# Linear attention with each head's decayed queries in a column block of their own, the other head's rows zero

## The chip, the cores and the metric

The kernel runs on one core of a Trainium2 chip. The metric is the device time of one execution in microseconds (us). The core has five engines that run side by side: TensorE (PE; its weight loads are listed apart as PEld), VectorE (DVE), ScalarE (ACT), GpSimd (POOL) and SyncE (SP), which here issues the transfers. TensorE multiplies a stationary operand, loaded as weights, with a moving operand that streams through column by column; the contraction runs over the partitions, that is the rows of its array, and results go to PSUM.

## The reference

Two layers of a hybrid block over 256 context and 1024 latent positions. Each layer projects a normalized input, runs three branches (gated linear attention, grouped-query attention, a recurrent branch) and merges them. The change is in the first branch, in fp32 throughout:

```python
q_dec = q * jnp.exp(g_cum)
k_inv = k * jnp.exp(-g_cum)
k_tail = k * jnp.exp(g_last - g_cum)
lower = jnp.tril(jnp.ones((GLA_CHUNK, GLA_CHUNK), bool))
a = jnp.where(lower, jnp.einsum('bhncd,bhnsd->bhncs', q_dec, k_inv), 0.0)
o = jnp.einsum('bhncs,bhnse->bhnce', a, v)
u = jnp.einsum('bhncd,bhnce->bhnde', k_tail, v)
decay = jnp.exp(g_last[:, :, :, 0, :])
...
o = o + jnp.einsum('bhncd,nbhde->bhnce', q_dec, s_in)
```

There are 4 heads with 64 key and 128 value elements, each run forward and backward over the positions; the two directions are added, normalized and gated.

## The kernel before, in words

`hybrid_kernel` goes through the two layers (L339). In a layer the linear attention comes early. For each pair of heads (`for g in range(2)`, L657) `gla_proj` (L528) makes queries `rq`, keys `rk` and values `v` for the pair, and `gla_core` (L541) does the attention. `weave` (L203) emits the core with high priority and puts attention projections (`att_proj`, L649) between its steps; the order on every engine's queue is then planned for the whole program from the emitted order, the priorities and estimated times. Behind the second pair come the projections of the recurrent branch (`rwkv_proj`), the attention, the recurrent branch itself (`gram`, `merge`, `chain`) and the merge of the branches.

In the core a pair of heads lies on the partitions: head 0 on rows 0 to 63, head 1 on rows 64 to 127, and the 1280 positions along the columns. For each direction `d`, the cumulated gates `G` are made, their exponentials `Ep` and `Em` (L575, L576), the decayed queries `qd[d]` (L584) and keys `kd[d]` (L585). For d = 0 these are tiles of their own; for d = 1 the queries are multiplied in place in `rq`, the keys in `rk`. `kt` is the transposed keys, and `R[d]` the states at the start of each tile of 128 positions, built one tile after the other on TensorE, VectorE and GpSimd (L596 to L603).

Then the tile loop (L605) goes over the tiles of 128 positions: 10 in layer 0, the 8 latent ones in layer 1, so with two pairs 36 tiles in all. Per tile:

- queries times keys, L616 to L620: for each direction and head a product on the head's 64 rows, [64 x 128] by [64 x 128], into the columns 128d of one PSUM buffer per head (`pa`);
- the mask, L622: one VectorE instruction per head, both directions, into `aT`;
- `aT` times values, L627, on 128 rows, into one PSUM buffer per head (`po`);
- queries times state, L631, on the head's 64 rows, added into the same buffer;
- the norm and the gate (L633 to L638), two transposes of the result `gth` through PSUM `u` (L642), a scaled copy, and the transfer to memory (L646).

The PSUM tag `a` has two buffers (L115), which `pa` and `po` and the state products take in turn. Fp32 products appear in the trace as two MATMUL instructions each, transposes as one; all products are recorded under L85 and all transposes under L90, the lines of the helper class.

Of the kernel before, what the change touches and what calls it, by code (L numbers as in the profile page):

```python
# [9 lines left out]
F32 = mybir.dt.float32  # L10
F32R = mybir.dt.float32r
AF = mybir.ActivationFunctionType
ALU = mybir.AluOpType
# [7 lines left out]
NT = CTX + SEQ  # L21
# [49 lines left out]
def hybrid_kernel(ctx: ExitStack, tc: tile.TileContext, I: dict, C: dict, out: bass.AP):  # L71
# [3 lines left out]
    vec = nc.vector  # L75
    pool = nc.gpsimd
# [16 lines left out]
    pe = PE  # L93

    def nm(s):
        cnt[0] += 1
        return f"{s}{cnt[0]}"
# [3 lines left out]
    def popen(**kw):  # L101
        g = tc.tile_pool(bufs=1, reuse_waits="tile", **kw)
        open_pools.append(g)
        return g, g.__enter__()
# [12 lines left out]
    def ps(tag):  # L117
        return psp.tile([128, 512], F32, tag=tag, bufs=PSB[tag], name=nm("ps_" + tag))
# [7 lines left out]
    def dense():  # L126
        ring["i"] += 1
        return ps(ring["tags"][(ring["i"] - 1) % len(ring["tags"])])
# [18 lines left out]
    for j in range(2):  # L147
        vec.tensor_scalar(
            out=sil[:, :, j, :], in0=cth[:, j, :].unsqueeze(2).to_broadcast([128, 8, 16]),
# [189 lines left out]
    for l in range(DEPTH):  # L339
# [57 lines left out]
        def th512():  # L397
            return ta.tile([128, 512], F32, tag="th", bufs=3, name=nm("th"))
# [22 lines left out]
        if l + 1 < DEPTH:  # L421
            mpool, mp = popen(name=nm("modp"))
            md, _ = modulation(l + 1, mp, 2)
# [83 lines left out]
        gpool, gp_ = popen(name=nm("gp"))  # L507
        glow, ge = popen(name=nm("ge"))
# [3 lines left out]
        amask = gp_.tile([128, 256], F32, name="amask")  # L512
# [15 lines left out]
        def gla_proj(pr):  # L528
# [9 lines left out]
                pass  # L538
            return qk, vt

        def gla_core(pr, qk, vt):  # L541
            qd, kd, R = {}, {}, {}
            for d in range(2):
                G = ge.tile([128, NT], F32, tag="G", bufs=2, name=nm("G"))
                for (t0, n) in BLK:
                    pz = ps("a")
                    pe.matmul(pz[:, :n], wup[96:128, d, 128 * pr:128 * pr + 128], wd[96:128, t0:t0 + n], start=True, stop=True)
                    ab = ge.tile([128, 512], F32, tag="ab", bufs=1, name=nm("ab"))
                    act(out=ab[:, :n], in_=pz[:, :n], func=AF.Abs, bias=bz[:, d, pr:pr + 1])
                    act(out=ab[:, :n], in_=ab[:, :n], func=AF.Exp, scale=-1.0)  # L550
                    act(out=ab[:, :n], in_=ab[:, :n], func=AF.Ln, bias=1.0)
                    mn = th512()
                    vec.tensor_scalar(out=mn[:, :n], in0=pz[:, :n], scalar1=bz[:, d, pr:pr + 1], scalar2=0.0, op0=ALU.add, op1=ALU.min)
                    pool.tensor_tensor(out=mn[:, :n], in0=mn[:, :n], in1=ab[:, :n], op=ALU.subtract)
                    go, gi = G[:, t0:t0 + n], mn[:, :n]
                    if d:
                        go, gi = go[:, ::-1], gi[:, ::-1]
                    for i in range(0, n, 128):
                        vec.tensor_tensor_scan(out=go[:, i:i + 128], data0=one.to_broadcast([128, 128]), data1=gi[:, i:i + 128], initial=0.0, op0=ALU.mult, op1=ALU.add)
                    yield 0.5  # L560
                G3 = G.rearrange("p (t c) -> p t c", c=128)
                mid = 64 if d else 63
                last = 0 if d else 127
                em = small.tile([128, NTILE, 1], F32, tag="em", bufs=2, name=nm("em"))
                act(out=em, in_=G3[:, :, mid:mid + 1], func=AF.Exp, scale=1.0 / 16)
                vec.tensor_copy(out=(gm := small.tile([128, NTILE, 1], F32, tag="gm", bufs=2, name=nm("gm"))), in_=G3[:, :, mid:mid + 1])
                vec.tensor_tensor(out=G3, in0=G3, in1=gm.to_broadcast([128, NTILE, 128]), op=ALU.subtract)
                if d == 0:
                    qd[d] = Ep = gp_.tile([128, NT], F32, tag="qd", name=nm("qd"))
                    kd[d] = Em = gp_.tile([128, NT], F32, tag="kd", name=nm("kd"))  # L570
                else:
                    Ep = ge.tile([128, NT], F32, tag="G", bufs=2, name=nm("E"))
                    Em = G
                    qd[d], kd[d] = qk["q"], qk["k"]
                act(out=Ep, in_=G, func=AF.Exp, scale=1.0 / 16)  # L575
                act(out=Em, in_=G, func=AF.Exp, scale=-1.0 / 16)  # L576
                order = list(range(NTILE)) if d == 0 else [1, 0] + list(range(9, 1, -1))
                cf = small.tile([128, NTILE, 1], F32, tag="cf", bufs=2, name=nm("cf"))
                eL = Ep.rearrange("p (t c) -> p t c", c=128)[:, :, last:last + 1]
                for i in range(NTILE - 1):  # L580
                    a, b = order[i], order[i + 1]
                    vec.tensor_tensor(out=cf[:, a], in0=eL[:, a], in1=em[:, b], op=ALU.mult)
                q0 = 0 if need_ctx else CTX
                vec.tensor_tensor(out=qd[d][:, q0:], in0=Ep[:, q0:], in1=qk["q"][:, q0:], op=ALU.mult)  # L584
                vec.tensor_tensor(out=kd[d], in0=Em, in1=qk["k"], op=ALU.mult)  # L585
                kt = ge.tile([128, NTILE, 128], F32, tag="G", bufs=2, name=nm("kt"))
                for t0 in range(0, NTILE, 4):
                    m = min(4, NTILE - t0)
                    pt = ps("u")
                    for i in range(m):  # L590
                        pe.transpose(pt[:, 128 * i:128 * i + 128], kd[d][:, 128 * (t0 + i):128 * (t0 + i) + 128], ident)
                    act(out=kt[:, t0:t0 + m, :].rearrange("p t c -> p (t c)"), in_=pt[:, :128 * m], func=AF.Copy)
                    yield 0.5
                R[d] = gp_.tile([128, NTILE, 128], F32, tag=f"R{d}", name=nm("R"))
                vec.memset(R[d][:, order[0], :], 0.0)
                for i in range(NTILE - 1):  # L596
                    a, b = order[i], order[i + 1]
                    pu = ps("a")
                    for h in range(2):
                        pe.matmul(pu[64 * h:64 * h + 64, 0:128], kt[:, a, 64 * h:64 * h + 64], vt[:, a, 128 * h:128 * h + 128], start=True, stop=True)  # L600
                    rt = ge.tile([128, 128], F32, tag="rt", bufs=1, name=nm("rt"))
                    vec.tensor_tensor(out=rt, in0=pu[:, 0:128], in1=R[d][:, a, :], op=ALU.add)
                    pool.tensor_scalar(out=R[d][:, b, :], in0=rt, scalar1=cf[:, a], scalar2=None, op0=ALU.mult)  # L603
                    yield 0.45
            for t in tiles:  # L605
                c = slice(128 * t, 128 * t + 128)
# [4 lines left out]
                pool.tensor_scalar(out=yo, in0=yo, scalar1=1.0, scalar2=None, op0=ALU.add)  # L611
                vec.reciprocal(out=yo, in_=yo)
                pool.tensor_tensor(out=th, in0=th, in1=yo, op=ALU.mult)
                aT = gp_.tile([128, 2, 256], F32, tag="aT", bufs=2, name=nm("aT"))

                pa = [ps("a"), ps("a")]  # L616
                for d in range(2):
                    for h in range(2):
                        r = slice(64 * h, 64 * h + 64)
                        pe.matmul(pa[h][:, 128 * d:128 * d + 128], kd[d][r, c], qd[d][r, c], start=True, stop=True)  # L620
                for h in range(2):
                    vec.scalar_tensor_tensor(out=aT[:, h], in0=pa[h][:, 0:256], scalar=3e38, in1=amask, op0=ALU.min, op1=ALU.mult)  # L622
                po = [ps("a"), ps("a")]
                for h in range(2):
                    vv = vt[:, t, 128 * h:128 * h + 128]
                    for d in range(2):
                        pe.matmul(po[h][:, 0:128], aT[:, h, 128 * d:128 * d + 128], vv, start=d == 0, stop=False)  # L627
                for d in range(2):
                    for h in range(2):
                        r = slice(64 * h, 64 * h + 64)  # L630
                        pe.matmul(po[h][:, 0:128], qd[d][r, c], R[d][r, t, :], start=False, stop=d == 1)  # L631
                ss = small.tile([128, 2], F32, tag="ss2", name=nm("ss2"))
                for h in range(2):  # L633
                    act(out=yo[:, 128 * h:128 * h + 128], in_=po[h][:, 0:128], func=AF.Square, accum_out=ss[:, h:h + 1])
# [22 lines left out]
        for g in range(2):  # L657
            banks("mm", "mm", "o")
            pj = gla_proj(g)
            banks("mm", "mm", "o")  # L660
            weave(gla_core(g, *pj), att_proj(g), 1.0, None, 3000)
# [632 lines left out]
        for bi, wo in enumerate(("w_o_gla", "w_o_att", "w_o_rwkv")):  # L1294
            if bi == 2:
                mb = blocks_of(blks)
            for jj in range(4):
                wh, wl = load_w([I[wo][l, :, 256 * jj:256 * jj + 256]], kt=4)
                for j in range(2):
                    kr = 2 * jj + j  # L1300
                    w = slice(128 * j, 128 * j + 128)
                    for (t0, n) in blks:
                        th = ta.tile([128, 512], F32, tag="th", bufs=4, name=nm("th"))[:, :n]
                        dma(out=th, in_=tg[bi][128 * kr:128 * kr + 128, t0:t0 + n])
                        p = dense()[:, :n]
# [115 lines left out]
```

## Time and profile before

| | us |
|---|---|
| median of 3 runs | 3962.02 |
| lowest, highest | 3959.33, 3962.11 |
| the profiled execution | 3955.01 |
| its span, first to last instruction | 3953.2 |

| engine | busy us | share of the span |
|---|---|---|
| PE (matmul) | 3698.9 | 94% |
| PEld (weight load) | 3092.6 | 78% |
| DVE | 2100.1 | 53% |
| ACT | 1761.0 | 45% |
| POOL | 604.9 | 15% |

The mean granted clock of TensorE was 0.962 of its full speed. Busy time says how long an engine had something under way; matmuls are pipelined, so their durations overlap, and what one costs is read from the start of one to the start of the next. A row of the timeline merges neighbours of the same kind (x4): its start is that of the first, its duration reaches to the end of the last. In a PE row `ps_a<-qd,kd 64*128 64x128`, the part before the arrow is what is written, `64*128` are the array's rows and columns in use, `64x128` the moving operand.

### The profile page before, as it was taken

The numbers are of one execution on the slowest core, as the hardware profiler recorded it, in microseconds if no ns is written. First come the engines' busy times: TensorE is split into PE (matmuls) and PEld (weight loads), VectorE is DVE, ScalarE is ACT, GpSimd is POOL, SyncE is SP. The second block draws the span as 40 slices with busy tenths as digits, with TensorE's granted clock in tenths as the row PEclk, the third lists the DMA queues.
The fourth block names the chain that finished last, engine by engine and source line by source line (L and its number), as shares of the span: only waits on it lengthen the run. The fifth ranks groups of instructions, "written<-read, shape, count | busy, mean of one in ns | idle before, by whom it ended". The sixth has DMA issues, their size and how long they took to land.

```text
span 3953.2 us, 81725 instructions
## 1 busy us (share of the span) xinstructions
PE 3698.9 (94%) x31928; PEld 3092.6 (78%) x31928; DVE 2100.1 (53%) x5083; ACT 1761.0 (45%) x4099; POOL 604.9 (15%) x714
## 2 busy tenths in 40 slices
PE   4999999999979989999999999999999899999899
PEld 2799887887767778777888899877878677777687
DVE  3234344437865766664453244444378676666562
ACT  3244437437843444344234344365388333343422
POOL 1133230001200000000233142300022000000042
PEclk7999999999989999999999999999999899999999
DMA  7723222426786777755644232224376676675653
GB/s 221 254 59 88 58 77 96 141 72 186 243 210 138 167 178 178 168 136 162 182 147 137 75 88 79 67 81 128 97 245 202 166 167 162 147 176 119 175 165 116
DMA packets 870964, 568.53 MB, mean 144 GB/s; under 512 B 307568, under 2 KB 775344, under 8 KB 868528
## 3 DMA queue, kind: packets, MB, share of 16 engines
q1 hardware_dynamic: 870576, 563.29, 51.7%
q8 instruction: 251, 4.11, 0.4%
q14 instruction: 137, 1.12, 0.1%
HBM read 379.86 MB, written 183.26 MB: 142 GB/s over the span
## 4 chain that ended last, share of the span: by engine, by line
PE 63%; DMA 14%; DVE 9%; ACT 7%; issue 4%; SPq 2%; POOL 0%; POOLq 0%; DVEq 0%; ACTq 0%
PE ps_mm L85 25%; PE ps_a L85 17%; PE ps_o L85 11%; PE ps_u L85 5%; PE ps_t L85 3%; DMA nscr<-Ms 2%; PE ps_t L90 2%; DMA Lm<-nscr 2%; DMA wr<-in_w_in_dram 1%; DMA tscr<-acc 1%; ACT L158 1%; DMA DT<-tscr 1%; DVE acc L1042 1%; DVE mt L1039 1%; DVE wl L349 1%
## 5 line engine op out<-in xcount | busy, mean ns | idle before, releaser
L85 PE MATMUL ps_mm<-h,wh 128*128 128x512 f32 (+1 forms) x2496 | 759.1, 386 | 14.8 <-DVE rk L683 6.7
L85 PEld LDWEIGHTS ps_mm<-h,wh 128*128 128x128 f32 x2496 | 448.6, 194 | 107.1 <-DVE rk L683 7.8
L349 DVE TENSOR_TENSOR wl<-wr,wh 128x512 fp32r<-128x512 f32 (+1 forms) x464 | 326.9, 726 | 293.1 <-ACT wh L348 287.8
L85 PE MATMUL ps_mm<-h,wl 128*128 128x512 f32 (+1 forms) x1248 | 471.0, 378 | 0.7 <-DVE wl L349 0.7
L348 ACT ACTIVATE wh<-wr 128x512 fp32r<-128x512 f32 (+1 forms) x464 | 271.9, 620 | 394.4 <-PE ps_mm L85 131.2
L85 PE MATMUL ps_mm<-wh,h 128*128 128x256 f32 x2032 | 403.5, 291 | 11.7 <-ACT wh L348 5.6
L85 PEld LDWEIGHTS ps_mm<-wh,h 128*128 128x128 f32 x2032 | 329.1, 195 | 27.3 <-issue 9.8
L85 PE MATMUL ps_a<-h,wh 128*128 128x512 f32 (+1 forms) x1024 | 297.6, 372 | 5.7 <-DVE rk L683 3.6
L85 PE MATMUL ps_mm<-wl,h 128*128 128x256 f32 x1016 | 294.1, 290 | 0.9 <-DVE wl L349 0.9
L85 PE MATMUL ps_o<-h,wh 128*128 128x512 f32 (+1 forms) x928 | 284.9, 388 | 1.1 <-DVE M L1315 1.0
L85 PEld LDWEIGHTS ps_mm<-h,wl 128*128 128x128 f32 x1248 | 241.4, 193 | 47.2 <-issue 4.2
L85 PEld LDWEIGHTS ps_a<-h,wh 128*128 128x128 f32 x1024 | 184.9, 191 | 37.7 <-DVE rk L683 4.4
L85 PEld LDWEIGHTS ps_mm<-wl,h 128*128 128x128 f32 x1016 | 197.6, 195 | 7.8 <-issue 4.9
L85 PE MATMUL ps_o<-wh,h 128*128 128x256 f32 x976 | 197.1, 289 | 2.5 <-ACT h L289 1.2
L1071 POOL COPY T<-Dg 128x512 f32<-128x512 f32 x40 | 28.5, 712 | 1087.8 <-DMA Dg<-dscr 842.4
L85 PEld LDWEIGHTS ps_o<-h,wh 128*128 128x128 f32 x928 | 165.2, 194 | 35.1 <-issue 2.2
L85 PE MATMUL ps_a<-h,wl 128*128 128x512 f32 (+1 forms) x512 | 190.9, 373 | 0.0
L1039 DVE TENSOR_TENSOR mt<-Lm,acc 64x15 f32<-64x15 f32 (+2 forms) x600 | 120.1, 200 | 118.6 <-DMA Lm<-nscr 93.9
L85 PE MATMUL ps_o<-h,wl 128*128 128x512 f32 (+1 forms) x464 | 174.6, 376 | 1.2 <-DVE wl L349 1.2
L85 PEld LDWEIGHTS ps_o<-wh,h 128*128 128x128 f32 x976 | 158.4, 192 | 8.9 <-issue 4.3
L85 PE MATMUL ps_t<-AR,BK 64*128 64x128 f32 x1280 | 127.7, 301 | 25.4 <-DVE BK L992 14.4
L85 PEld LDWEIGHTS ps_t<-AR,BK 64*128 64x128 f32 x1280 | 102.5, 196 | 56.9 <-issue 39.5
(341 smaller groups left out, 7847.6 us busy)
## 6 DMA issues: line engine op xcount, KB each, us to landing
wr<-in_w_in_dram SPq DMA_DIRECT2D x376, 256.0 KB, 3.9
tg<-th SPq DMA_DIRECT2D x96, 256.0 KB, 3.9
th<-tg SPq DMA_DIRECT2D x96, 256.0 KB, 3.0
wm<-in_w_mod_dram SPq DMA_DIRECT2D x16, 1024.0 KB, 7.1
ld_kk<-rscr_kk SPq DMA_DIRECT2D x40, 256.0 KB, 5.0
ld_dc<-rscr_dc SPq DMA_DIRECT2D x40, 256.0 KB, 4.7
ld_ka<-rscr_ka SPq DMA_DIRECT2D x40, 256.0 KB, 5.4
ld_kd<-rscr_kd SPq DMA_DIRECT2D x40, 256.0 KB, 5.4
```

Of the source, the lines that this page charges most:

```text
L85: PE.last = nc.tensor.matmul(*a, **k)
L90: PE.last = nc.tensor.transpose(*a, **k)
L158: act(out=dst, in_=src, func=AF.Ln, scale=scale, bias=bias)
L348: act(out=hi, in_=src, func=AF.Copy)
L349: vec.tensor_tensor(out=lo, in0=src, in1=hi.bitcast(F32), op=ALU.subtract)
L1039: vec.tensor_tensor(out=mt[:, :n, :w], in0=Lm[:, j, j + 1:16].unsqueeze(2).to_broadcast([64, n, w]), in1=acc[:, j:j + 1, :w].to_broadcast( ...
L1042: vec.tensor_tensor(out=acc[:, j + 1:16, :w], in0=acc[:, j + 1:16, :w], in1=mt[:, :n, :w], op=ALU.add)
L1071: pool.tensor_copy(out=T.rearrange("p d m t -> p (d m t)"), in_=Dg.rearrange("p d m t -> p (d m t)"))
```

## The change

Two tiles `qd` of two column blocks each, one block per head, are made once per layer and filled with zeros on GpSimd. The decayed queries of head h are written to its own 64 rows of block h, by one VectorE instruction per head, so that block h holds zeros on the other head's rows. Queries times keys is then one product per direction, over all 128 rows of `kd[d]`, with both blocks as 256 moving columns, into one PSUM buffer for both directions. `aT` is ordered by direction, and the mask instruction goes by direction with the mask repeated over the heads. Queries times state stays one product per direction and head, now over 128 rows. The forward exponential is made in the ring of `G`, and the backward queries no longer overwrite `rq`. SBUF holds two tiles of 10 KB per partition in place of one of 5 KB.

```diff
--- before.py
+++ after.py
@@ -538,8 +538,13 @@
                 pass
             return qk, vt
 
+
+        qd = [gp_.tile([128, 2, NT], F32, name=nm("qd")) for _ in range(2)]
+        for d in range(2):
+            pool.memset(qd[d], 0.0)
+
         def gla_core(pr, qk, vt):
-            qd, kd, R = {}, {}, {}
+            kd, R = {}, {}
             for d in range(2):
                 G = ge.tile([128, NT], F32, tag="G", bufs=2, name=nm("G"))
                 for (t0, n) in BLK:
@@ -566,12 +571,12 @@
                 vec.tensor_copy(out=(gm := small.tile([128, NTILE, 1], F32, tag="gm", bufs=2, name=nm("gm"))), in_=G3[:, :, mid:mid + 1])
                 vec.tensor_tensor(out=G3, in0=G3, in1=gm.to_broadcast([128, NTILE, 128]), op=ALU.subtract)
                 if d == 0:
-                    qd[d] = Ep = gp_.tile([128, NT], F32, tag="qd", name=nm("qd"))
+                    Ep = ge.tile([128, NT], F32, tag="G", bufs=2, name=nm("E"))
                     kd[d] = Em = gp_.tile([128, NT], F32, tag="kd", name=nm("kd"))
                 else:
                     Ep = ge.tile([128, NT], F32, tag="G", bufs=2, name=nm("E"))
                     Em = G
-                    qd[d], kd[d] = qk["q"], qk["k"]
+                    kd[d] = qk["k"]
                 act(out=Ep, in_=G, func=AF.Exp, scale=1.0 / 16)
                 act(out=Em, in_=G, func=AF.Exp, scale=-1.0 / 16)
                 order = list(range(NTILE)) if d == 0 else [1, 0] + list(range(9, 1, -1))
@@ -581,7 +586,9 @@
                     a, b = order[i], order[i + 1]
                     vec.tensor_tensor(out=cf[:, a], in0=eL[:, a], in1=em[:, b], op=ALU.mult)
                 q0 = 0 if need_ctx else CTX
-                vec.tensor_tensor(out=qd[d][:, q0:], in0=Ep[:, q0:], in1=qk["q"][:, q0:], op=ALU.mult)
+                for h in range(2):
+                    r = slice(64 * h, 64 * h + 64)
+                    vec.tensor_tensor(out=qd[d][r, h, q0:], in0=Ep[r, q0:], in1=qk["q"][r, q0:], op=ALU.mult)
                 vec.tensor_tensor(out=kd[d], in0=Em, in1=qk["k"], op=ALU.mult)
                 kt = ge.tile([128, NTILE, 128], F32, tag="G", bufs=2, name=nm("kt"))
                 for t0 in range(0, NTILE, 4):
@@ -611,24 +618,22 @@
                 pool.tensor_scalar(out=yo, in0=yo, scalar1=1.0, scalar2=None, op0=ALU.add)
                 vec.reciprocal(out=yo, in_=yo)
                 pool.tensor_tensor(out=th, in0=th, in1=yo, op=ALU.mult)
-                aT = gp_.tile([128, 2, 256], F32, tag="aT", bufs=2, name=nm("aT"))
-
-                pa = [ps("a"), ps("a")]
+                aT = gp_.tile([128, 2, 2, 128], F32, tag="aT", bufs=2, name=nm("aT"))
+                pa = ps("a")
                 for d in range(2):
-                    for h in range(2):
-                        r = slice(64 * h, 64 * h + 64)
-                        pe.matmul(pa[h][:, 128 * d:128 * d + 128], kd[d][r, c], qd[d][r, c], start=True, stop=True)
-                for h in range(2):
-                    vec.scalar_tensor_tensor(out=aT[:, h], in0=pa[h][:, 0:256], scalar=3e38, in1=amask, op0=ALU.min, op1=ALU.mult)
+                    pe.matmul(pa[:, 256 * d:256 * d + 256], kd[d][:, c], qd[d][:, :, c], start=True, stop=True)
+                for d in range(2):
+                    vec.scalar_tensor_tensor(
+                        out=aT[:, d], in0=pa[:, 256 * d:256 * d + 256].rearrange("p (h i) -> p h i", h=2), scalar=3e38,
+                        in1=amask[:, 128 * d:128 * d + 128].unsqueeze(1).to_broadcast([128, 2, 128]), op0=ALU.min, op1=ALU.mult)
                 po = [ps("a"), ps("a")]
                 for h in range(2):
                     vv = vt[:, t, 128 * h:128 * h + 128]
                     for d in range(2):
-                        pe.matmul(po[h][:, 0:128], aT[:, h, 128 * d:128 * d + 128], vv, start=d == 0, stop=False)
+                        pe.matmul(po[h][:, 0:128], aT[:, d, h], vv, start=d == 0, stop=False)
                 for d in range(2):
                     for h in range(2):
-                        r = slice(64 * h, 64 * h + 64)
-                        pe.matmul(po[h][:, 0:128], qd[d][r, c], R[d][r, t, :], start=False, stop=d == 1)
+                        pe.matmul(po[h][:, 0:128], qd[d][:, h, c], R[d][:, t, :], start=False, stop=d == 1)
                 ss = small.tile([128, 2], F32, tag="ss2", name=nm("ss2"))
                 for h in range(2):
                     act(out=yo[:, 128 * h:128 * h + 128], in_=po[h][:, 0:128], func=AF.Square, accum_out=ss[:, h:h + 1])
```

## Rows read from the trace of the kernel before

**Rows 1.** Page, part 1: busy us (share of the span) xinstructions of each engine.

```profile
PE 3698.9 (94%) x31928; PEld 3092.6 (78%) x31928; DVE 2100.1 (53%) x5083; ACT 1761.0 (45%) x4099; POOL 604.9 (15%) x714
```

**Rows 2.** Windows: start:end, length, busy us of PE, PEld, DVE, ACT, POOL, clock, DMA.

```profile
300.00:430.00 130.00, 130.00 (x1000) 117.90 (x999) 63.95 (x137) 60.88 (x237) 46.92 (x73) 1.00 0.33 91
...
600.00:660.00 60.00, 56.83 (x300) 45.78 (x300) 28.66 (x58) 40.67 (x76) 4.76 (x6) 0.94 0.29 95
2240.00:2440.00 200.00, 200.00 (x1533) 181.06 (x1533) 89.19 (x207) 87.08 (x320) 71.69 (x108) 1.00 0.28 78
...
2540.00:2660.00 120.00, 114.60 (x675) 95.58 (x675) 48.70 (x105) 65.77 (x134) 11.12 (x14) 0.96 0.24 73
1060.00:1860.00 800.00, 729.36 (x9211) 594.26 (x9209) 501.35 (x1319) 347.97 (x713) 40.64 (x45) 0.93 0.69 167
3100.00:3700.00 600.00, 556.44 (x7782) 437.61 (x7783) 393.61 (x1095) 231.54 (x471) 23.96 (x26) 0.94 0.67 151
```

**Rows 3.** Instructions on the tile qd: engine, operation, count, ns min/median/max, forms.

```profile
L85 PE MATMUL ps_a<-qd,kd x144: 272/373/576, 300.6 to 2637.4; 64*128 64x128 f32 x144
```

**Rows 4.** Timeline of PE, a group of four: start us, us, instructions in order.

```profile
304.42 0.28 PE L85 MATMUL ps_o<-wh,h 128*128 128x256 f32 x1
304.54 0.60 PE L85 MATMUL ps_a<-v,aT 128*128 128x128 f32 x4
305.07 0.48 PE L85 MATMUL ps_a<-R,qd 64*128 64x128 f32 x2
...
305.93 0.28 PE L85 MATMUL ps_o<-wl,h 128*128 128x256 f32 x1
```

**Rows 5.** Timeline of PE, queries times keys cut by a transpose.

```profile
344.17 0.27 PE L90 MATMUL ps_u<-c_ident,gth 128*128 128x128 f32 x1
344.38 0.48 PE L85 MATMUL ps_a<-qd,kd 64*128 64x128 f32 x2
344.79 0.33 PE L90 MATMUL ps_u<-c_ident,gth 128*128 128x128 f32 x1
345.05 0.37 PE L85 MATMUL ps_a<-qd,kd 64*128 64x128 f32 x1
345.06 0.37 PE L85 MATMUL ps_a<-rq,rk 64*128 64x128 f32 x1
...
346.03 0.28 PE L85 MATMUL ps_o<-wl,h 128*128 128x256 f32 x1
```

**Rows 6.** Timeline of PE, a group of eight.

```profile
348.43 1.05 PE L85 MATMUL ps_a<-v,aT 128*128 128x128 f32 x8
349.41 0.49 PE L85 MATMUL ps_a<-R,qd 64*128 64x128 f32 x4
...
350.28 0.28 PE L85 MATMUL ps_mm<-wl,h 128*128 128x256 f32 x1
```

**Rows 7.** Timeline of PE, full-row fp32 products of 256 columns.

```profile
678.19 0.59 PE L85 MATMUL ps_t<-th,c_oblk 128*128 128x256 f32 x2
678.43 0.47 PE L85 MATMUL ps_a<-h,wl 128*128 128x256 f32 x1
678.74 0.40 PE L85 MATMUL ps_a<-h,wh 128*128 128x256 f32 x2
```

**Rows 8.** Timeline of PE, 32-row fp32 products of 256 columns.

```profile
172.58 0.69 PE L85 MATMUL ps_a<-wd,wup 32*128 32x256 f32 x2
173.21 0.66 PE L90 MATMUL ps_t<-c_ident,bA 128*128 128x128 f32 x4
```

**Rows 9.** Instructions of lines 584 and 764: count, ns min/median/max, forms.

```profile
L584 DVE TENSOR_TENSOR qd<-qd,rq x4: 1227/1360/1493, 205.5 to 2444.1; 128x1280 f32<-128x1280 f32 x2, 128x1024 f32<-128x1024 f32 x2
...
L764 DVE TENSOR_TENSOR up<-raw,up x8: 687/689/981, 903.6 to 2883.8; 64x512 fp32r<-64x512 f32 x8
```

**Rows 10.** Waits of PE: who waited for whom, us in total, times, longest.

```profile
PE ps_u L90 <- DVE gth L638: 6.2, 2, 4.2
```

**Rows 11.** Instructions of line 1071: count, ns min/median/max, forms.

```profile
L1071 POOL COPY T<-Dg x40: 609/614/2639, 1175.8 to 3686.0; 128x512 f32<-128x512 f32 x40
```

## The prediction

> **What bounds the kernel now.** I read the page's busy shares first: the TensorE matmuls are busy 94% of the span, the VectorE 53%, the GpSimd 15% [rows 1]. That is an average, so next comes the windows view for the stages that the change touches. The decayed queries are used only in the tile loop of `gla_core`, which runs four times: about 300 to 405 us and 530 to 655 us (layer 0, head pairs 0 and 1), 2335 to 2420 and 2540 to 2660 us (layer 1). In the two pair-0 stretches PE is busy for the whole of the window at a granted clock of 1.00, that is 2.4 GHz; where a pair-1 loop ends it is busy 56.83 of 60 and 114.60 of 120 us, at 0.94 and 0.96 [rows 2]. VectorE is busy about half of the first of these windows and GpSimd about a third. So PE's stream is the bound there: the core loop has its own chain (products, mask, products, norm, transposes), but projections fill PE between its steps. What PE saves in these loops should move the end; what other engines gain or lose should not.
>
> How PE spends the loop is then read in the timeline, from start to start, because matmuls are pipelined and durations overlap. First the pitches. One fp32 product is two MATMUL instructions: 144 of them for the 36 tiles' forward keys and queries of both heads [rows 3], and as many each for the backward ones and for queries times state in each direction. Eight 128-row instructions of 128 columns take 1.05 us and four 0.60, so they come 0.11 us apart [rows 4, 6], and what follows a projection's of 256 columns starts 0.12 us after it [rows 4]. Two full-row fp32 instructions of 256 columns with one projection instruction behind them take 0.55 us, so (0.55 - 0.12)/2 = 0.215 us each [rows 7].
>
> **What the change removes.** I cost each group of 64-row instructions as the time from the start of the work before it to the second start behind it, less the pitches of its neighbours.
> - One head alone, four instructions: 305.93 - 304.54 = 1.39, less 4 x 0.11 and 0.12, is **0.83 us** [rows 4]. Only 0.44 of it is columns; the rest is bare time before and behind the group, about 0.2 us on either side.
> - Both heads in turn, eight instructions: 350.28 - 348.43 = 1.85, less 8 x 0.11 and 0.12, is **0.85 us** [rows 6]; most repeats lie at 0.84. Eight cost what four do, since the two heads' instructions sit on different halves of the rows and run together: the starts of neighbours differ by 0.01 us [rows 5].
> - Queries times keys cut in two by a transpose, two and then six: 346.03 - 344.17 = 1.86, less two transposes (0.22) and two projection instructions (0.24), is **1.40 us** [rows 5].
>
> Going through the PE timeline of the four loops in this way gives 22 of the 36 tiles with the cut pattern for queries times keys, 4 with two groups of four, 10 with one of eight; for queries times state 5 tiles with two groups of four, 31 with one of eight. Together: 22 x 1.40 = 30.8, 18 groups of four x 0.83 = 14.9, 41 groups of eight x 0.84 = 34.4, sum **80.1 us**.
>
> **What it puts there.** Per tile, queries times keys become two products of 128 rows and 256 columns, four instructions x 0.215 = 0.86 us; queries times state stay four products of 128 columns, now on 128 rows, eight instructions x 0.11 = 0.88 us. 36 x 1.74 = **62.6 us**. Nothing is added around them: the products of `aT` and `v`, also fp32 on 128 rows, start 0.12 us after the projection instruction before them [rows 4], and the keys' products will stand as they do. Saving: 80.1 - 62.6 = **17.5 us**. It comes from the cut and the four-groups; each group of eight by itself loses 0.04 us or less. By pairs it is some 10 us in the two pair-0 loops, where PE has no gap at all, and some 7 us in the pair-1 loops, where it has a few per cent of gaps; I take 17 us as landing.
>
> The unknown here is the full-row price. From above, a 256-column fp32 pair on a part of the rows takes 0.63/2 = 0.315 us each, with the switches around it [rows 8]; at that price the keys' products cost 144 x 0.10 = 14 us more and the saving is 3. From below, at the projections' 0.12 us it would be 14 us more. I take 0.215, the row with the same type, rows and columns.
>
> **The other engines.** VectorE: each of the eight query multiplies becomes two, one per half of the partitions. A 128-partition one takes 1.23 to 1.49 us, and 64 partitions with 512 elements take 0.689 us, which for 1024 to 1280 elements is 1.4 to 1.7 us, so halving the partitions saves nothing [rows 9]. That is 8 x 1.4 = 11 us more VectorE work and 1.4 us more in the chain before each state recurrence. I cost it at nothing: PE is full there with projections; without that cover it is 11 us. The forward exponential moves into the two-buffer ring of G; the next direction's G then waits for these multiplies instead of for the second exponential, a matter of the same 1 to 3 us, under the same cover.
>
> The mask step stays two instructions of 256 columns, but the first head's `aT` products now need both, one VectorE step more in each tile's chain. Against that the next tile's keys' products need one PSUM buffer, where two had to come free. I count both as nothing; PE waited for this chain's last step 6.2 us in all, in two places [rows 10], which bounds what a shorter chain could add and shows where a longer one would be seen. The raw queries are no longer overwritten, so their buffer comes free earlier, but keys and values still hold the next pair back, and PE has no gap there.
>
> GpSimd: four zero fills of 2560 columns. The nearest row is a copy of 512 columns at 0.614 us, so about 3.1 us each [rows 11]. They stand before the GLA projections. Hidden, they cost nothing; if all four were put ahead of the subtractions that build the projections' input on the same queue, with the instructions behind them waiting, 12 us. SyncE's queue gets no transfer more or less.
>
> **Sum.** The profiled execution took 3955.0 us (3953.2 span and 1.8 around it), 7.0 under the median 3962.0 of the runs. 3955.0 - 17 = 3938; against the median, which I forecast, 3962 - 17 = **3945 us**.
>
> **The rivals.**
> 1. *The exposed time stays* (slower). The 0.2 us on either side of a group might not belong to the 64-row form but to fp32 operands of the queries. Then 72 groups keep 0.40 us: 28.8 - 17.5 = 11 us slower, 3973. It wins no time from 0.24 us a group on, and is slower by more than the bound from 0.35. Against it: the `aT` products have no such time before them [rows 4]. 5%.
> 2. *The halves already run together* (slower). If a pair on two halves cost one instruction's columns and nothing else, the 576 old instructions would be 288 x 0.11 = 31.7 us, and 62.6 for the new ones is 31 us slower, 3993. The 0.01 us starts speak for the mechanism [rows 5], the measured 0.84 for a group of 0.44 of columns against its price [rows 6]. 2%. The Trainium skill ("TensorE: Matmul & The Clock Gate", Part 3: Packing small matmuls) has this rule: matmuls with few rows, placed in distinct row groups, run concurrently, so it would speak against padding. The trace agrees on the concurrency and charges the switch besides.
> 3. *The gain lands by half or less*. In the pair-1 loops and behind them PE waits for VectorE and ScalarE at times; if those 7 us are lost, or the 0.315 us price holds, or the zero fills delay the projections, 3 to 7 us of gain are left: 3955 to 3959. For it: the clock and gaps in the last windows [rows 2]. 18%.
> 4. *The planner's order shifts*. The order on all queues is planned for the whole program with estimated times, so other instruction sizes here can reorder the recurrent stages later, where PE has 70.6 us of gaps in 800 and 43.6 in 600 [rows 2]. Slower by more than the bound needs 25 us more gaps there, a fifth more: 3975, 7%. The same luck the other way: under 3930, 6%.
>
> **How the numbers follow.** The forecast (62%) has 3945, by itself 3934 to 3954. The range 3930 to 3963 takes in rival 3 and leaves out rival 4's better end and the slower cases, some 20%. A measurement of this kernel can tell about 0.2%, 7.9 us, from no change, so faster means under 3954.1: 62 + 6 = 68%; within: 18%; slower: 5 + 2 + 7 = 14%.
>
> **What would show it.** Right: in the timeline the keys' products stand as four instructions 0.215 us apart with no 0.2 us before or behind; queries times state as eight at 0.11 us, 0.88 us in all; PE still full in the pair-0 windows; the start of the second layer's first loop earlier by about 10 us. Wrong: bare time beside the new groups (rival 1); a pitch near 0.3 us; PE idle within the pair-0 loops behind VectorE's mask step; zero fills in front of the input's subtractions; or equal time saved by 700 us that is gone again behind the recurrent stages (rival 4).

## The result and the profile after

The changed kernel took **4013.41 us**, median of 4 runs (4011.25 to 4022.46), against 3961.77 for the kernel before on the same chip: a ratio of **1.0141 [1.0126, 1.0156]** (in brackets the 95% interval; the ratios compare all runs of both kernels and can differ by about 0.1% from the quotient of the medians). It is 52 us slower; the forecast was 3945, and the range ended at 3963. The profiled execution took 4022.46 us (span 4020.7), 67 us more than the one before.

The page's busy shares, part 1, of the kernel after; beside them stand [rows 1]:

```profile
PE 3720.3 (93%) x31784; PEld 3126.3 (78%) x31784; DVE 2113.8 (53%) x5091; ACT 1732.5 (43%) x4077; POOL 614.2 (15%) x718
```

PE issues 144 instructions fewer and is busy 21 us longer. Where, the windows of the after kernel show (start:end, length; busy us of PE, PEld, DVE, ACT, POOL; granted clock; DMA):

```profile
300.00:430.00 130.00, 128.76 (x991) 122.16 (x989) 64.84 (x139) 60.99 (x238) 47.92 (x75) 1.00 0.32 91
520.00:560.00 40.00, 39.47 (x312) 37.40 (x311) 12.17 (x25) 12.19 (x41) 6.20 (x9) 1.00 0.27 79
560.00:600.00 40.00, 25.34 (x119) 21.01 (x117) 14.69 (x24) 10.77 (x45) 7.14 (x9) 0.79 0.16 46
600.00:640.00 40.00, 33.22 (x151) 27.62 (x152) 13.74 (x40) 13.80 (x35) 2.30 (x3) 0.83 0.29 89
2340.00:2440.00 100.00, 100.00 (x821) 96.53 (x820) 47.10 (x107) 46.09 (x192) 41.26 (x69) 1.00 0.37 104
2580.00:2620.00 40.00, 30.83 (x180) 26.98 (x179) 15.05 (x26) 11.50 (x43) 6.51 (x8) 0.86 0.21 59
2620.00:2660.00 40.00, 31.82 (x138) 26.66 (x137) 14.98 (x40) 14.39 (x41) 3.15 (x4) 0.76 0.31 96
```

and the same view of the kernel before, in layer 0's second-pair loop:

```profile
520.00:560.00 40.00, 40.00 (x319) 35.92 (x318) 11.24 (x32) 10.84 (x39) 7.85 (x13) 1.00 0.26 76
560.00:600.00 40.00, 39.78 (x250) 33.63 (x249) 18.18 (x34) 18.21 (x43) 4.75 (x6) 1.00 0.22 66
600.00:640.00 40.00, 38.47 (x222) 31.48 (x221) 19.22 (x37) 27.27 (x53) 4.76 (x6) 1.00 0.25 79
```

The first-pair loops (first and fifth row after) are full or nearly so, as in [rows 2]. In the second-pair loops PE, which had been full to 600 us, is busy 25.34 us of 40, and its granted clock falls to 0.79. Half as many PE instructions run there (119 for 250), and ScalarE is busy 10.77 us for 18.21: work has left this stretch.

The timeline of PE says which (after; start us, us, instructions in order, in brackets the idle time before and what ended it):

```profile
563.80 1.06 PE L85 MATMUL ps_a<-R,qd 128*128 128x128 f32 x8
568.49 0.45 PE L90 MATMUL ps_u<-c_ident,gth 128*128 128x128 f32 x1 [3.62 <-DVE gth L643]
568.72 1.06 PE L85 MATMUL ps_a<-qd,kd 128*128 128x256 f32 x2
569.58 1.06 PE L85 MATMUL ps_a<-qd,rk 128*128 128x256 f32 x2
570.43 0.42 PE L90 MATMUL ps_u<-c_ident,gth 128*128 128x128 f32 x1
571.15 2.08 PE L85 MATMUL ps_a<-v,aT 128*128 128x128 f32 x8 [0.30 <-DVE aT L626]
...
610.06 2.04 PE L85 MATMUL ps_a<-v,aT 128*128 128x128 f32 x8 [0.30 <-DVE aT L626]
611.93 1.06 PE L85 MATMUL ps_a<-R,qd 128*128 128x128 f32 x8
614.58 0.59 PE L90 MATMUL ps_u<-c_ident,gth 128*128 128x128 f32 x2 [1.58 <-DVE gth L643]
616.77 0.79 PE L85 MATMUL ps_mm<-h,wh 128*128 128x512 f32 x1 [1.60 <-DVE rk L688]
```

From 563 us on nothing stands between the steps of the loop: no `ps_mm<-h,wh`, which are the recurrent branch's projections (`rwkv_proj`), until the last tile is through. Two blocks of these projections, one of 256 and one of 512 columns, had been multiplied before; their first and last instructions:

```profile
553.46 0.40 PE L85 MATMUL ps_mm<-h,wh 128*128 128x256 f32 x2
562.68 0.40 PE L85 MATMUL ps_mm<-h,wl 128*128 128x512 f32 x1
```

The PSUM tag `mm` has two buffers (L115), so both are then full, and the third block (616.77, the last row before these) waits for the instruction on `rk` that empties the first of them. So the branch's first products were there in time; what came late is their way out of PSUM. Every step of the loop's chain is bare, above all the norm (3.62 us to `gth`). The instructions on `u` show the same: ScalarE's evictions of the recurrent projections (count; ns min/median/max; first and last start; forms), kernel before and after, 500 to 720 us:

```profile
L682 ACT ACTIVATE u<-ps_mm,mu x18: 455/668/690, 564.6 to 692.5; 128x512 f32<-128x512 f32 x12, 128x256 f32<-128x256 f32 x6
```

```profile
L687 ACT ACTIVATE u<-ps_mm,mu x18: 458/668/697, 615.7 to 711.1; 128x512 f32<-128x512 f32 x12, 128x256 f32<-128x256 f32 x6
```

The first eviction comes 51 us later in layer 0 (615.7 for 564.6), 3.6 us behind the last products that read `aT` (group of 610.06, ends at 612.1). In layer 1 the same row begins at 2642.7 instead of 2563.2.

**The theories.** A, the *overlap*: the change makes the tiles of pool `gp_` 15 KB per partition larger. What is allocated behind them moves up, and now the second buffer of `aT`, read to the loop's end, reaches into the place of the first `rk` tile of `rwkv_proj` (`shifted`, pool `sp`, which grows from the other end). That tile can't be written before `aT` has been read for the last time (`u` lies clear of it, but its part and `rk`'s empty the same PSUM buffer). The addresses in the built programs, KB per partition, here with those of the experiments:

| kernel | second `aT` | pool `ge` | first `rk` of `shifted` |
|---|---|---|---|
| before | 65.25 to 67.25 | 67.25 to 86.8 | 81.91 to 86.91 |
| after | 80.25 to **82.25** | 82.25 to 101.8 | 81.91 to 86.91 |
| `rq` moved to `ge` (e1) | 75.25 to 77.25 | 77.25 to 101.8 | 81.91 to 86.91 |
| before, pad of 15 KB (e2) | 80.25 to **82.25** | 82.25 to 101.8 | 81.91 to 86.91 |
| before, pad of 14 KB (e3) | 79.25 to 81.25 | 81.25 to 100.8 | 81.91 to 86.91 |

The overlap is 352 bytes. `ge` overlaps with `rk` in every version, but its tiles are done before the loop: the last state step starts at 528.8 us before and 525.6 after. The rivals: A2, the larger overlap with `ge` is what costs; B, the new instructions themselves hold the loop up (the mask that the first head's products wait for, the halves on VectorE), whatever the addresses; and C, the *planned order* of later stages, rival 4 of the prediction.

### The profile page after: what moved, and what is told of

Same layout as the page of the kernel before. It is cut to its first block, busy times and chain, and to the rows that moved or that the text cites. A ratio compares the mean times of both kernels' runs of the same rounds, so it can differ in the third digit from the quotient of the medians.

```text
span 4020.7 us, 81469 instructions
## 1 busy us (share of the span) xinstructions
PE 3720.3 (93%) x31784; PEld 3126.3 (78%) x31784; DVE 2113.8 (53%) x5091; ACT 1732.5 (43%) x4077; POOL 614.2 (15%) x718
## 5 line engine op out<-in xcount | busy, mean ns | idle before, releaser
L85 PE MATMUL ps_mm<-h,wh 128*128 128x512 f32 (+1 forms) x2496 | 754.8, 385 | 15.5 <-DVE rk L688 6.2
L85 PEld LDWEIGHTS ps_mm<-wl,h 128*128 128x128 f32 x1016 | 196.7, 194 | 6.8 <-issue 4.4
L903 POOL TENSOR_TENSOR y<-y,sg 128x128 f32<-128x128 f32 x64 | 36.1, 564 | 810.9 <-DVE y L902 664.1
```

Source lines behind the costliest of these rows:

```text
L85: PE.last = nc.tensor.matmul(*a, **k)
L903: pool.tensor_tensor(out=y[:, hc], in0=y[:, hc], in1=sg[:, hc], op=ALU.mult)
```

## The experiments

**The overlap without the change, and the change without the overlap.** e1 is the changed kernel with 5 KB moved from `gp_` to `ge`; e2 and e3 are the kernel before with an unused tile of 15 or of 14 KB:

```diff
-                qk[nme] = gp_.tile([128, NT], F32, tag="r" + nme, name=nm("r" + nme))
+                qk[nme] = (ge if nme == "q" else gp_).tile([128, NT], F32, tag="r" + nme, name=nm("r" + nme))
```

```diff
         gn = gp_.tile([128, 4], F32, name="gn")
+        pad = gp_.tile([128, 3840], F32, name=nm("pad"))   # 3584 in e3
+        pool.memset(pad[:, 0:1], 0.0)
```

> The changed kernel, but the raw queries rq (5 KB, last read before the tile loop) are taken from the pool ge instead of gp_, so that the mask tiles aT end at 77.25 KB in place of 82.25 and the first tile of the recurrent branch's projections (rk, from 81.9 KB) no longer lies on one of them. Theory A (the loss is this overlap of 352 bytes: the projections cannot fill PE during the second pair's tile loop): the projections' first result comes at about 560 us instead of 616, PE is full in 560 to 600 us, and the time is the forecast of the products alone, 3945 us (ratio 0.996; 0.993 to 0.999). Theory B (the loss belongs to the new products or to the order planned around them): about 4010 us (ratio 1.01) as in the changed kernel. In between, near 3980: part of each.

> The kernel before with an unused tile of 15 KB in the pool gp_, so that its tiles stand where the changed kernel's do and aT ends at 82.25 KB, over the first 352 bytes of rk; the products are the old ones. Theory A: as slow as the changed kernel plus the products' 17 us, about 4025 us (ratio 1.016; 1.010 to 1.022), the projections' first result only behind the last tile of the second pair. Theory B: the same as before, 3962 us.

> The kernel before with an unused tile of 14 KB: aT ends at 81.25 KB, short of rk, while the pool ge, whose tiles are done with before the tile loop, lies under the projections' tiles as in the changed kernel. Theory A: no loss, 3962 us within 10 (ratio 0.998 to 1.003). A second theory A2 (the overlap with ge, 20 KB, is what costs): about as slow as with 15 KB, 4020 us. Theory B: 3962 us.

e1: 3967.25 us against 3953.62, 1.0039 [1.0023, 1.0054]. e2: 4052.77, **1.0256 [1.0241, 1.0271]**. e3: 3954.85, 1.0007 [0.9996, 1.0018]. One KB of unused space more, and the old kernel loses 2.5%; e3, in which `ge` lies over nearly as much of the branch's tiles and nothing is lost, ends A2. Windows of e1, e2 and e3 in this order (columns as above), to be held against 39.78 and 25.34 busy in the same stretch:

```profile
560.00:600.00 40.00, 40.00 (x228) 35.06 (x227) 20.33 (x39) 20.22 (x44) 5.01 (x6) 1.00 0.29 93
```

```profile
560.00:600.00 40.00, 34.94 (x162) 27.41 (x160) 15.45 (x27) 11.67 (x43) 7.15 (x9) 0.72 0.22 62
600.00:640.00 40.00, 33.20 (x127) 26.16 (x127) 14.57 (x38) 13.20 (x36) 2.29 (x3) 0.64 0.28 86
```

```profile
560.00:600.00 40.00, 39.78 (x250) 33.64 (x248) 17.78 (x33) 18.38 (x44) 4.75 (x6) 1.00 0.22 66
```

and the first evictions of the recurrent projections, e1 and e2:

```profile
L687 ACT ACTIVATE u<-ps_mm,mu x18: 457/668/689, 556.3 to 684.2; 128x512 f32<-128x512 f32 x12, 128x256 f32<-128x256 f32 x6
```

```profile
L684 ACT ACTIVATE u<-ps_mm,mu x17: 456/669/694, 622.6 to 711.2; 128x512 f32<-128x512 f32 x11, 128x256 f32<-128x256 f32 x6
```

e2 has none of the new instructions, and its branch starts at 622.6 us; e1 has all of them, and starts at 556.3, 8 us ahead of the kernel before, with PE full. That shows A and ends rival B. e2's loss was larger than expected (2.56% for 1.6). Three things go that way, and they were not separated: the 64-row groups in a bare loop, a clock of 0.64 to 0.72, and a later order of layer 1, of which more below. The part in layer 0 is free of that order: its end, the last instruction on `xs`, stands at 2206.7 us in e2 and at 2159.4 in e3, 47 us apart.

e1 missed its expectation too: without the overlap it was to be 0.4% faster than before and is 0.4% slower. Layer 0 gains: its end stands at 2142.3 us, 15.5 ahead of the kernel before (2157.8), where the prediction had about 10. So a second loss lies in layer 1.

**Which layer.** e4 has the new core in layer 0 alone, e5 in layer 1 alone, both with `rq` in `ge` where the core is new:

```diff
+        wide = l == 0        # l == 1 in e5
-            weave(gla_core(g, *pj), att_proj(g), 1.0, None, 3000)
+            weave((gla_core if wide else gla_core_old)(g, *pj), att_proj(g), 1.0, None, 3000)
```

> The changed products (with rq in ge) in layer 0 alone; layer 1 computes with the old ones. The planned order of layer 1's attention tail and recurrent stage is then that of the kernel before, where the version with both layers changed has one attention tile fewer done when the recurrent branch's last inputs are made. Theory C (the products give 10 us in the pair-0 loop and a few in the pair-1 loop of layer 0, and the loss that is left in the version with rq in ge is layer 1's order): the gain of layer 0 reaches the end, ratio 0.996 (0.993 to 0.998), some 16 us. Theory D (the rest of the loss goes with the products in either layer): ratio 1.00 to 1.003.

> The changed products (with rq in ge) in layer 1 alone. The planned order of layer 1's tail is the other one, as in the version with both layers changed. Theory C: 8 us gained in the loops and some 25 lost between the end of the attention and the fifth recurrent step, ratio 1.004 (1.002 to 1.007). Theory D: half of the version with both layers, ratio 1.002, with no loss at that place.

e4: 3939.84 us against 3954.20, **0.9977 [0.9964, 0.9989]**. e5: 3975.12, **1.0061 [1.0045, 1.0077]**. Both lie in the ranges expected with C, and they add up to e1 (-0.23 and +0.61 are +0.38%; e1 +0.39). In layer 0 the change brings 9 us (4 to 14 by the interval); in layer 1 the same change costs 24. The loss comes behind the loops: counted from the last input of the recurrent branch (the last `z`), the fifth step of its state chain (`T`) is copied 183.5 us later in the kernel before and 183.0 in e4, but 212.2 in e1 and 214.8 in e5. From that step to the end all take alike (723 to 731 us). What these kernels share is the planned order on SyncE's queue: in before, e3 and e4, 14 of layer 1's 16 attention tiles (`yTatt`) are stored ahead of the last transfer into the branch's `bR`; in e1, e2, e5 and the changed kernel 13.

**The order put back.** `weave` merges attention into the recurrent branch's preparation by a ratio; 0.14 for 0.12 in layer 1 puts the attention tile back to where it was (14 of 16). e6 does so on e1, e7 on the kernel before, where the order is as it was already:

```diff
-        weave(rw, att, 0.12, to_end=False)
+        weave(rw, att, (0.12, 0.14)[l], to_end=False)
```

> Both layers changed, rq in ge, and in layer 1 attention is woven into the recurrent branch's projections at 0.14 in place of 0.12, so that 14 of 16 attention tiles are done where the kernel before has 14 and the version without this has 13. Theory C: the loss behind the attention of layer 1 goes, ratio 0.994 (0.991 to 0.998). Theory D: 1.004 as without it.

> The kernel before with the same 0.14 in layer 1, as a comparison for the run above. It is planned with 14 of 16 tiles there with either number. Theory C: ratio 1.000 (0.997 to 1.003); if it is below 0.998, a part of what the version above gains is the weaving's.

e6: 3931.62 us, **0.9954 [0.9940, 0.9968]**, 18 us faster than the kernel before, and the fastest of all. e7: 3950.13, 0.9995 [0.9984, 1.0006], so the ratio alone gives nothing; against e7, e6 is 16 to 19 us faster. Windows of e1 and then e6 in the stretch of those first steps:

```profile
3040.00:3240.00 200.00, 175.19 (x1796) 140.56 (x1795) 124.28 (x343) 65.49 (x137) 7.79 (x7) 0.85 0.62 148
```

```profile
3040.00:3240.00 200.00, 184.25 (x2079) 149.07 (x2077) 140.27 (x388) 78.38 (x167) 7.90 (x10) 0.94 0.72 171
```

the last `z` (first row of each pair) and the copies of the first five steps (second row; columns as for `u`), kernel before, e1, e6:

```profile
L792 ACT ACTIVATE z<-ps_a,prm x48: 457/687/729, 2889.8 to 3043.2; 128x512 f32<-128x512 f32 x32, 128x256 f32<-128x256 f32 x16
L1071 POOL COPY T<-Dg x5: 613/616/2639, 3144.1 to 3226.7; 128x512 f32<-128x512 f32 x5
```

```profile
L797 ACT ACTIVATE z<-ps_a,prm x48: 453/684/718, 2866.5 to 3017.5; 128x512 f32<-128x512 f32 x32, 128x256 f32<-128x256 f32 x16
L1076 POOL COPY T<-Dg x5: 611/617/4357, 3126.0 to 3229.7; 128x512 f32<-128x512 f32 x5
```

```profile
L797 ACT ACTIVATE z<-ps_a,prm x48: 455/677/730, 2871.5 to 3031.3; 128x512 f32<-128x512 f32 x32, 128x256 f32<-128x256 f32 x16
L1076 POOL COPY T<-Dg x5: 611/618/2093, 3122.4 to 3205.5; 128x512 f32<-128x512 f32 x5
```

e1 starts the chain 18 us ahead of the kernel before and has lost all of it by the fifth step (103.7 us for 82.6); e6 keeps it. This shows C: e1 and e6 differ in one number of the order, worth 0.85%. How a later attention tile stretches these steps wasn't isolated: the attention ends 49 us behind the last `z` in e1 and 31 in e6, so more of it lies beside the first steps, and PE runs at a lower clock there (0.85 for 0.94). In the kernel before and e4 it ends 42 us behind.

**How much of it is in the changed kernel.** e8 is the changed kernel again, e9 the same with e6's edit.

> The changed kernel once more, to have it beside the next run on one chip: ratio 1.014 (1.012 to 1.020 on either theory).

> The changed kernel, its tiles where the change puts them (aT over the first 352 bytes of rk), with layer 1's attention woven in at 0.14, which alone brought the version without the overlap down by 0.85%. Theory C (two losses apart from each other: the overlap and layer 1's planned order): the order's part goes, here 16 us by the time from the last input of the recurrent branch to the fifth recurrent step (199.8 us in the changed kernel, 183.5 before), ratio 1.010 (1.006 to 1.013), and what stays is the overlap's. If the overlap alone made the order's loss, the ratio stays at 1.014; if the order were all of it, it falls to 0.996.

e8: 4010.21 us against 3952.23, 1.0145 [1.0127, 1.0162]. e9: 4002.22, 1.0123 [1.0092, 1.0154]. The intervals overlap, so by the times C's part in the changed kernel stays open, between nothing and some 0.6%. The traces, one execution each, narrow it. In e9 the fifth step comes 173.2 us behind the last `z`, where the changed kernel has 199.8 and e8 196.7, but the last `z` itself, counted from the end of layer 0, comes 10 to 16 us later. From the end of layer 0 to the fifth step the changed kernel takes 1101.7 us, e8 1093.2 and e9 1085.2: the order costs 8 to 16 us there, against 27 without the overlap (e1 1087.4, e6 1060.4).

That the overlap stands without C is shown by e9 against e6, both with the order put back: 1.0123 / 0.9954 = 1.017, about 67 us (54 to 81 by the intervals; each is held against the kernel before on its own chip). With the changed kernel's order in both, e8 against e1, it is 1.0145 / 1.0039 = 1.011, 42 us (33 to 51). So the two losses don't simply add; together they are 1.0145 / 0.9954 = 1.019, some 75 us. Most of the overlap's part falls in layer 0, which ends 40 to 48 us later with it (2185.6 for 2145.1 in e9 and e6; 2189.8 and 2184.8 for 2142.3 in the changed kernel, e8 and e1). e9's window (columns as above) has the hole where the changed kernel has it:

```profile
560.00:600.00 40.00, 24.96 (x118) 20.61 (x116) 14.62 (x25) 10.74 (x45) 7.88 (x10) 0.79 0.15 45
```

## Why the prediction was wrong, and where it was right

**The products: right.** The timeline of PE in the changed kernel, where projections lie beside the loop:

```profile
527.60 0.28 PE L85 MATMUL ps_mm<-wl,h 128*128 128x256 f32 x1
527.72 0.59 PE L85 MATMUL ps_a<-qd,kd 128*128 128x256 f32 x2
528.15 0.59 PE L85 MATMUL ps_a<-qd,rk 128*128 128x256 f32 x2
528.39 0.47 PE L85 MATMUL ps_mm<-wh,h 128*128 128x256 f32 x1
528.70 0.28 PE L85 MATMUL ps_o<-wh,h 128*128 128x256 f32 x1
...
350.95 0.83 PE L85 MATMUL ps_a<-v,aT 128*128 128x128 f32 x6
351.62 1.06 PE L85 MATMUL ps_a<-R,qd 128*128 128x128 f32 x8
352.43 0.36 PE L85 MATMUL ps_mm<-wl,h 128*128 128x256 f32 x1
352.63 0.40 PE L85 MATMUL ps_mm<-wh,h 128*128 128x256 f32 x2
```

Read as [rows 4 to 6] were: keys' products 528.70 - 527.72 less 0.12 are 0.86 us, queries times state 352.63 - 351.62 less 0.12 are 0.89; forecast 0.86 and 0.88. Two of the keys' instructions start 0.43 us after the first two, so 0.215 each. No bare time stands before or behind them, so rival 1 falls: the 0.2 us belonged to the 64-row form. The Trainium skill ("TensorEngine Tiling (Array Packing)", Key Properties) says that a change of the tiling mode drains the engine. The trace agrees: [rows 4] have some 0.2 us on either side of a 64-row group, and the full-row products have none. Rival 2 falls with e6: its price would have made the products 31 us slower.

**The other engines: right.** The multiplies on half of the partitions and the zero fills (after, lines 591 and 544, columns as for `u`):

```profile
L591 DVE TENSOR_TENSOR qd<-E,rq x16: 1207/1388/1490, 206.8 to 2544.3; 64x1280 f32<-64x1280 f32 x8, 64x1024 f32<-64x1024 f32 x8
```

```profile
L544 POOL MEMSET qd<- x4: 2227/2232/2240, 185.0 to 2217.2; 128x2560 f32 x4
```

Sixteen, at 1.21 to 1.49 us as long as a whole one in [rows 9]; the fills took 2.2 us for the estimated 3.1 [rows 11]. e6 has them and is still 18 us faster, as much as the products alone were to bring, so no cost of theirs is seen.

**The saving: right in size, not in this kernel, and in part by luck.** 17.5 us were summed; e6 against the kernel before is 18 (13 to 24 by the interval), against e7 16 to 19. Only e6 realises it. The split is not as summed: about 10 us were to fall in layer 0, and its end comes 12 to 20 us earlier (2139.8 to 2145.1 us in e1, e4 and e6; 2156.6 to 2159.4 in the kernel before, e3, e5 and e7), which by the middle values leaves layer 1 less than its 7. Why wasn't isolated.

**The step that failed** is "I take 17 us as landing". It rested on the sentence that projections fill PE between the steps of the loop. The halves were put at nothing by that cover, and the longer chain to the first `aT` products because PE had waited only 6.2 us for the chain's end, which holds under the same cover. But what lets the cover's own work start and leave PSUM was never followed back. The text on the change names what the sum has no term for: two tiles of 10 KB in place of one of 5. Where PE in [rows 2] was busy 56.83 of the last 60 us, it is 33.22 of 40 in the changed kernel, behind a stretch of 25.34. The prediction's own mark for a wrong chain was PE's wait for `gth`, 6.2 us in 2 places [rows 10]; in the after kernel's waits (total, times, longest) it is

```profile
PE ps_u L90 <- DVE gth L643: 26.4, 12, 3.6
```

With the overlap each tile's chain is bare; the prediction had priced that only for VectorE's part ("without that cover it is 11 us"). The price was 42 us in the changed kernel's order and 67 with the order put back. The Trainium skill has the sign of it ("Perfetto Trace Analysis", Optimization Strategy): the same gap repeating for a stretch on the engine that should be full can mean that there isn't enough SBUF or PSUM for the next tile to be allocated. The trace after agrees (the `gth` gap 12 times); here it was the place of the tiles and not their amount, since 5 KB moved ended it (e1). No row of the kernel before could have shown it, only the addresses.

**Rival 4** named the right mechanism for the second loss, an order planned anew from other instruction sizes, at a fifth more gaps in the recurrent stage or 25 us. e1 against e6 shows it at 0.85%, 34 us, in the first steps of layer 1's chain. It had 7%, and it wasn't what made the changed kernel slower than the range: e9, without it, is still 1.2% slower than before. **Rival 3** (a part of the gain lost in the second-pair loops) looked at the right place, with too small a loss, since it asked how much of 7 us could be lost and not what else starts there.

## What to carry to other kernels

A change that makes a tile larger moves all that is allocated behind it: look at which tiles of the next stage come to lie on tiles that are read to the end of this one, and put at that border those that die early (5 KB moved from one pool to the other are worth 42 us here, e8 to e1, or 67, e9 to e6). Before a cost is put at nothing because other work covers it, follow that work back to what releases its first instruction, memory included. Padding to all rows of the array pays where groups on part of the rows stand alone or are cut, 18 us for 36 tiles here; and where an order is planned from estimates, compare the order of the later stages too before a gain is taken as landing.

## What was not expected of the hardware

An idle PE can cost twice. The same window view of the changed kernel for the stretch of the group at 568.72:

```profile
556.00:564.00 8.00, 8.00 (x45) 6.87 (x44) 2.98 (x7) 1.89 (x4) 0.00 (x0) 1.00 0.55 160
564.00:568.00 4.00, 0.86 (x8) 0.67 (x6) 1.58 (x1) 1.43 (x7) 0.85 (x1) 0.94 0.04 12
568.00:573.00 5.00, 4.21 (x14) 3.36 (x15) 1.35 (x5) 0.63 (x2) 0.73 (x1) 0.50 0.18 50
```

Behind the wait of 3.62 us the granted clock is 0.50, that is 1.2 GHz: the two keys' instructions of 568.72 and of 569.58 start 0.86 us apart where it was 0.43 at 527.72, and the eight `aT` products take 2.08 us for 1.05 [rows 6]. So where the clock is low, the bare loop loses not only the gaps: the products between them take double as well. This holds for a part of the loop only; the mean granted clock of 560 to 600 us is 0.79.
